# A second operand made from the x that is on chip: one core, two layers of a hybrid encoder

## The chip, the cores and the metric

One core of a Trainium2 chip runs the whole program. The metric is the device time of one execution in microseconds (us); the time before is the median of three runs.

## The reference

Two layers run over 512 frames of width 1024, all in fp32. Each layer has a first block with two branches, a feed-forward block, and a gated embedding. Cut to what matters here:

```python
for i in range(DEPTH):                       # DEPTH = 2
    h = rmsnorm(x, norm1_g[i])
    z = h @ w_in[i] + b_in[i]                # mLSTM q,k,v,o,i,f; retention q,k,v,g; gates gm, gr
    ...                                      # branch A: conv(q,k), mLSTM (4 heads), sig(o) * headnorm
    ...                                      # branch B: rotary q,k, retention (4 heads), silu(g) * headnorm
    merged = sigmoid(gm) * (y_m @ w_bm[i]) + sigmoid(gr) * (y_r @ w_br[i])
    x = x + merged @ w_out[i]
    h2 = rmsnorm(x, norm2_g[i])
    x = x + square(relu(h2 @ w_ff1[i] + b_ff1[i])) @ w_ff2[i] + b_ff2[i]
    h3 = rmsnorm(x, norm3_g[i])
    x = x + sigmoid(h3 @ w_pe_gate[i]) * (p[i] @ w_pe[i])
return rmsnorm(x, final_g)
```

## The kernel before

All activations lie transposed: x is eight tiles of 128 features by 512 frames (KT = 8, T = 512). Every fp32 operand of a matmul is split into a high and a low part in the matmul's reduced type, by a copy on ScalarE (ACT) and a subtraction on VectorE (DVE) (`split`, lines 262 and 263), and each product is three matmuls (`mm3`, lines 355 to 357). Weights stream in on the SyncE queue into a ring of four raw buffers and are split two units ahead of their use, into tiles wh and wl. `t8` is one output tile: eight k steps of three matmuls, 512 wide.

A group of eight projections (the retention queries, keys and gates, half of branch A's merge gates, all of branch B's, and the second feed-forward matrix) is done by pairs of tiles in a recursive seven-product scheme (`run_pair`). It needs sums and differences of quarters of the operand; for the branches these are the tiles xs (xsh, xsl), made by `xs_sums`, four batches of two tiles each.

In a layer's first block there are two versions of the normed x:

- The first operand xa is x times the norm's gain, without the norm's row factor (which is not known until all of x has been squared). Its results are multiplied by the row `n1.b` on the way out (the parameter `nrm`). It serves head 0, the values of heads 0 and 1, two branch gates (`gm_tile`) and head 1's queries and keys.
- The second operand xn is fully normed. `normed` loads a tile of x from memory on ACT's queue (line 935, tile xnr), multiplies it (line 936), and `xn_tile` splits it into xnh and xnl. Four tiles are made beside the two branch gates, four inside head 1's projection (lines 996 to 999). From head 0's output gates (`m_gates`) on, everything reads xn.
- `xs_sums` (lines 954 to 963) loads and multiplies x a second time (tile xsr), and all four batches stand behind the fourth head's values (lines 1028 and 1029).

`conv_evac` takes a query or key tile from PSUM: where `nrm` is given it multiplies it in place in PSUM (line 777), then ACT makes the first conv tap (line 778), and DVE adds three more (line 781).

At the end of the first block, `merged @ w_out` is added to x: line 1109 loads a tile of x into a temporary (xr), line 1111 adds, and the second norm's operand is made from the sum (n2h, n2l). After the last layer's gate the result is written out by `final`, which takes several tiles of x in one instruction.

Temporaries (`tmp`) come from a ring of NTMP = 6 tiles of 128x512 in this block; a tile is given out again when its last reader is done. The region "big" of 16 KB per partition holds x0, then the layer's xnh, then the layer's new x, each as one tile. The regions of xa, of xs and of the second norm's operand follow each other in one place.

The order on each engine is fixed when the program is built: a planner goes through the instructions in the order in which they are written, places them by its own estimate of times, and lets a later one go ahead where an earlier one can't start. In the trace, for instance, the loads of cos and sin (written behind the fourth head, line 1027) run in the first 10 us. GpSimd adds weight blocks in memory by DMA for the pair scheme, paced by the matmuls.

Of the kernel before, what the change touches and what calls it, by code (L numbers as in the profile page):

```python
# [35 lines left out]
F32 = mybir.dt.float32  # L36
F32R = mybir.dt.float32r
# [175 lines left out]
def build(ctx, tc, ins, out):  # L213
# [496 lines left out]
        return ct, em  # L710


    x = bpool.tile([P, KT, T], F32, name="x0", tag="big")
    xa_pool = phase("xa0", "right")
    cur["low"] = phase("low0", "left")
    cur["tmp"], cur["ntmp"] = cur["low"], NTMP
# [3 lines left out]
        te.matmul(warm[:, 0:P], ones, ones, start=True, stop=True)  # L720
    fill_raws(1)
    for k in range(KT):
        nc.sync.dma_start(x[:, k, :], ins["xT"][k])
    ready(0)
    for k in range(KT):
        n1.operand(k, x[:, k, :])
    nc.sync.dma_start(ident, ins["ident"])
    nc.sync.dma_start(bc[:, 1, :], ins["vecs"][1])

    for i in range(L):  # L730
# [37 lines left out]
            mm3(og, wh[:, s], wl[:, s], xa[0][k], xa[1][k], k == 0, k == KT - 1)  # L768
        if i == 0:
            for k in range(KT):  # L770
                n1.square(k, x[:, k, :])

        def conv_evac(o, nm, c, qh, ql, q, nrm):
            a = tmp(f"{nm}cv")
            cw = [bc[:, i, ow + 16 * j + c:ow + 16 * j + c + 1] for j in range(4)]
            if nrm:
                ve.tensor_tensor(o, o, nrm.b, OP.mult)
            ac.activation(a[:, :T], o, AF.Identity, bias=cbp[:, c:c + 1], scale=cw[3])
            for j in (2, 1, 0):
                t = slice(3 - j, T)  # L780
                ve.scalar_tensor_tensor(a[:, t], o[:, :T - 3 + j], cw[j], a[:, t], OP.mult, OP.add)
            ve.tensor_tensor(a[:, 0:3], a[:, 0:3], fix[:, :, c], OP.add)
            ac.activation(a[:, :T], a[:, :T], AF.Silu)
            if q:
                ac.activation(qh, a[:, :T], AF.Copy, scale=1.0 / 16)
                ve.scalar_tensor_tensor(ql, a[:, :T], 1.0 / 16, qh.bitcast(F32), OP.mult, OP.subtract)
            else:
                split(a[:, :T], qh, ql)
# [56 lines left out]
            head_scale(nm, num, 256, mv, hv)  # L845
            return num

        def m_gates(h):
            return [gated(f"l{i}m{h}o{v}", t8(xn, f"l{i}m{h}o{v}"), None, AF.Sigmoid, bcol(i, "bo", 2 * h + v))
                    for v in range(2)]  # L850

        def m_back(h, gs, num):
# [73 lines left out]
            nc.scalar.dma_start(gm_dram[i, c], g)  # L926


        big = bpool.tile([P, KT, T], F32R, name=f"l{i}xnh", tag="big")
        low = cur["br"].tile([P, KT, T], F32R, name=f"l{i}xnl", tag="xn")  # L930
        xn = [big[:, k, :] for k in range(KT)], [low[:, k, :] for k in range(KT)]

        def normed(nm, k):
            t = tmp(f"l{i}{nm}{k}")
            nc.scalar.dma_start(t, x_src[k])
            ve.scalar_tensor_tensor(t, t, n1.col(k), n1.b, OP.mult, OP.mult)
            return t

        def xn_tile(k):
            split(normed("xnr", k), xn[0][k], xn[1][k])  # L940

        def xs(k):
            def parts(j):
# [8 lines left out]
        xs = [xs(k) for k in range(4)]  # L952

        def xs_sums(k):
            t = [normed("xsr", 2 * k + a) for a in range(2)]
            u = [tmp(f"l{i}xsu{k}{a}") for a in range(2)]
            a, b = slice(0, S), slice(S, T)
            ve.tensor_tensor(u[0][:, a], t[0][:, b], t[0][:, a], OP.subtract)
            ve.tensor_tensor(u[0][:, b], t[1][:, a], t[0][:, a], OP.subtract)
            ve.scalar_tensor_tensor(u[1][:, a], u[0][:, b], -1.0, t[0][:, b], OP.mult, OP.subtract)  # L960
            ve.scalar_tensor_tensor(u[1][:, b], u[1][:, a], -1.0, t[1][:, b], OP.mult, OP.subtract)
            for a in range(2):
                split(u[a], xs_t[0][2 * k + a], xs_t[1][2 * k + a])
# [29 lines left out]
        gm = {}  # L993
        for c in range(2):
            gm_tile(c, xa, n1)
            xn_tile(2 * c)
            xn_tile(2 * c + 1)
        pt = m_scores(0, qk)
        qk = m_qk(1, xa, n1, lambda d: xn_tile(4 + d))
        xa_pool.release()  # L1000
        xs_pool = phase(f"xs{i}", act_side)
        shift(xs_pool, act_side, True)
        xs_t = acts(xs_pool, f"l{i}xs")
        shift(xs_pool, act_side, False)
        num = m_attend(0, pt, vv)
        gs = m_gates(0)
        gm_tile(2, xn, None)
        m_back(0, gs, num)
        pt = m_scores(1, qk)
        qk = m_qk(2, xn, None)  # L1010
        num = m_attend(1, pt, vv)
        gs = m_gates(1)
        vv = mv_vals(1, xn, None, lambda: m_back(1, gs, num))
        pt = m_scores(2, qk)
        qk = m_qk(3, xn, None)
        num = m_attend(2, pt, vv)
        gs = m_gates(2)
        gm_tile(3, xn, None)
        m_back(2, gs, num)
        pt = m_scores(3, qk)  # L1020
        gs = m_gates(3)
        num = m_attend(3, pt, vv)
        vv = rv_vals(0, lambda: m_back(3, gs, num))

        trig = [cur["low"].tile([P, T], F32, name=f"l{i}{n}", tag="trig", bufs=2) for n in ("cos", "sin")]
        for t, n in zip(trig, ("cos", "sin")):
            nc.scalar.dma_start(t, ins[n])
        for k in range(4):
            xs_sums(k)

        def bm_tile(c):
            if c < 4:
# [68 lines left out]
        xs_pool.release()  # L1101


        x = bpool.tile([P, KT, T], F32, name=f"l{i}x", tag="big")
        n2_pool = phase(f"n2{i}", act_side)
        n2 = Norm(f"l{i}n2", i, "g2", acts(n2_pool, f"l{i}n2"))
        for c in range(KT):
            xr = tmp(f"l{i}xr{c}")
            nc.scalar.dma_start(xr[:, :T], x_src[c])
            o = t8((mh, ml), f"l{i}wo{c}")  # L1110
            ve.tensor_tensor(x[:, c, :], o, xr[:, :T], OP.add)
            n2.tile(c, x[:, c, :])
        cur["low"].release()


# [28 lines left out]
            pair_operand(nm, st, *hid[b, p])  # L1144

        def tile3(c):
            n3.tile(c, x[:, c, :])

        def ff2(b, p):
            started = set()  # L1150

            def add(q, o, op):
                y = x[:, 2 * p + q // 2, (q % 2) * S:(q % 2 + 1) * S]
                if b == 0 and q not in started:
                    started.add(q)
                    ve.scalar_tensor_tensor(y, y, bcol(i, "bf2", 2 * p + q // 2), o, OP.add, op)
                else:
                    ve.tensor_tensor(y, y, o, op)

            def done(x_, o):  # L1160
                if x_ in ("P1", "P2"):
                    add(1, o, OP.add)
                elif x_ == "P5":
                    add(2, o, OP.subtract)
                elif x_ in ("P6", "P3"):
                    add(3, o, OP.subtract)
                elif x_ == "P7":
                    add(2, o, OP.subtract)
                elif x_ == "P4":
                    add(0, o, OP.add)  # L1170
                    if b == 3 and p == 3:
                        tile3(6)
                        tile3(7)
                if b == 3 and p and x_ in ("P6", "P7"):
                    tile3(2 * p - 2 + (x_ == "P7"))

            def parts(k):
                h, l = hid[b, k]
                return lambda j: (h[:, j * S:(j + 1) * S], l[:, j * S:(j + 1) * S])

            run_pair(f"l{i}o{b}{p}", [parts(k) for k in range(4)], done)
# [43 lines left out]
        def pe_evac(o, c, s, nn):  # L1225
            w = s.stop - s.start
            t = tmp(f"l{i}pgt{c}_{s.start}")[:, :w]
            ve.tensor_tensor(t, o[:, :w], n3.b[:, s], OP.mult)
            ac.activation(t, t, AF.Sigmoid)
            ve.tensor_tensor(t, t, pe[:, c, s], OP.mult)  # L1230
            ve.tensor_tensor(x[:, c, s], x[:, c, s], t, OP.add)
            for n in nn:
                if last:
                    n.square(c, x[:, c, :])
                else:
                    n.tile(c, x[:, c, :])

        for c in range(KT - LAST if last else KT):
            o = t8(n3.act, f"l{i}pg{c}")
            if c == 0:  # L1240
                n3.finish()
                held = o
                continue
            if c == 1:
                n3.spread()
                pe_evac(held, 0, slice(0, T), nn)
                if not last:
                    nc.scalar.dma_start(xs_dram[0], x[:, 0, :])
            pe_evac(o, c, slice(0, T), nn)
            if not last:  # L1250
                nc.scalar.dma_start(xs_dram[c], x[:, c, :])
        n1 = nn[0]
        if not last:
            cur["tmp"].release()
            n3_pool.release()

    def final(n, c0, c1):
        v = x[:, c0:c1, n.s]
        ve.tensor_tensor(v, v, n.b.rearrange("p (a t) -> p a t", a=1).to_broadcast([P, c1 - c0, n.n * P]), OP.mult)
        nc.sync.dma_start(out[c0:c1, :, n.s].rearrange("c p t -> p c t"), v)  # L1260

    for c in range(KT - LAST):
        ac.activation(x[:, c, :], x[:, c, :], AF.Copy, scale=nn[0].col(c))


    ws = [unit("T8") for _ in range(LAST)]
    for a, n in enumerate(nn):
        for c in range(KT - LAST, KT):
# [4 lines left out]
                mm3(o, wh[:, s], wl[:, s], n3.act[0][k][:, n.s], n3.act[1][k][:, n.s],  # L1273
                    k == 0, k == KT - 1)
            pe_evac(o, c, n.s, [n])
            ac.activation(x[:, c, n.s], x[:, c, n.s], AF.Copy, scale=n.col(c))
            if a == 1 and c == KT - LAST:
                nn[0].finish()
            elif a == 1 and c < KT - 1:
# [7 lines left out]
    cur["tmp"].release()  # L1287
    cur["last"].release()
    n3_pool.release()
    assert at["unit"] == NU and at["prep"] == len(order) and not pieces and not raws and at["load"] == len(order) and at["step"] == len(steps)  # L1290


# [111 lines left out]
```

## Time and profile before

| | before |
|---|---|
| median of three runs | 2447.42 us (2445.1 to 2448.85) |
| the profiled execution | 2447.46 us, span 2445.7 us |
| mean granted clock of TensorE | 0.983 |
| TensorE matmul busy | 97% |
| TensorE weight load busy | 86% |
| DVE busy | 65% |
| ACT busy | 49% |
| GpSimd busy | 10% |
| DMA | 481.9 MB, mean 197 GB/s |

Tile names carry the layer (l0, l1). PE is TensorE. In a row of the waits, the three numbers are the total wait in us, how often, and the longest. In a group of instructions stand busy us and mean ns, then the idle time of the engine before them and what ended it. A granted clock below 1.00 in a stretch means that TensorE ran part of it at half speed.

### The profile page before, as it was taken

Reading aid. Unit: us, or ns where it says so; the run is one execution under the profiler, and the core shown is the slowest. Engines: PE = TensorE matmul, PEld = TensorE weight load, DVE = VectorE, ACT = ScalarE, POOL = GpSimd, SP = SyncE. Lnnn points to the kernel's source line nnn. Section 1 sums busy time; section 2 is a strip of 40 time slices with the busy share of each in tenths; the row PEclk is TensorE's granted clock in tenths of the full one; section 3 lists DMA queues with packets and bytes.
Section 4 is the critical chain, followed back from the end, with each engine's and each line's share of the span. In section 5 each row is a group of like instructions: output and inputs, shape, how many; then the busy total and the mean of one; then the engine's idle time right before and its main releaser. Section 6 shows DMA issues by size and latency. Waiting matters only on the chain.

```text
span 2445.7 us, 35635 instructions
## 1 busy us (share of the span) xinstructions
PE 2378.4 (97%) x13788; PEld 2097.4 (86%) x13788; DVE 1589.8 (65%) x2451; ACT 1188.6 (49%) x1730; POOL 251.7 (10%) x368
## 2 busy tenths in 40 slices
PE   9899989999999999999999998999999999999997
PEld 7788878998998798899877886889989987998996
DVE  6766576774665577577777665667736655676675
ACT  5655443543454445445456552445535544455453
POOL 3121100000001100001301110000000010000012
PEclk9999999999999999999999999999999999999998
DMA  8666777668788777867767667776686884543441
GB/s 239 190 185 188 203 243 201 188 191 244 199 253 263 211 234 214 222 214 201 204 190 197 179 176 194 233 196 207 181 243 186 280 245 121 160 137 119 150 155 44
DMA packets 182187, 481.90 MB, mean 197 GB/s; under 512 B 18033, under 2 KB 20465, under 8 KB 182017
## 3 DMA queue, kind: packets, MB, share of 16 engines
q1 hardware_dynamic: 118512, 280.25, 34.5%
q0 software_dynamic: 41472, 159.39, 27.8%
q10 hardware_dynamic: 22032, 39.98, 4.7%
q8 instruction: 108, 1.77, 0.3%
q14 instruction: 63, 0.51, 0.1%
HBM read 464.87 MB, written 174.06 MB: 261 GB/s over the span
## 4 chain that ended last, share of the span: by engine, by line
PE 85%; DVE 5%; DMA 5%; issue 3%; ACT 1%; POOL 0%; ACTq 0%; POOLq 0%; DVEq 0%
PE l1f L356 2%; PE l1f L355 2%; PE l1f L357 2%; PE l0f L356 2%; PE l0f L357 2%; PE l0f L355 2%; PE l1br L357 1%; PE l0br L357 1%; PE l0br L355 1%; PE l1br L355 1%; PE l0br L356 1%; PE l1br L356 1%; DMA l1xsr<-x_spill 1%; DMA l1xr<-x_spill 1%; DMA l0xnr<-xT 1%
## 5 line engine op out<-in xcount | busy, mean ns | idle before, releaser
L262 ACT ACTIVATE wh<-wr 128x1024 fp32r<-128x1024 f32 x254 | 268.5, 1058 | 415.4 <-issue 46.1
L263 DVE TENSOR_TENSOR wl<-wr,wh 128x1024 fp32r<-128x1024 f32 x254 | 311.8, 1228 | 184.7 <-ACT wh L262 183.9
L262 ACT ACTIVATE wh_C<-wr 128x1024 fp32r<-128x1024 f32 x76 | 80.4, 1058 | 128.3 <-PE l0bm L356 8.8
L263 DVE TENSOR_TENSOR wl_B<-wr,wh_B 128x1024 fp32r<-128x1024 f32 x76 | 92.9, 1222 | 37.8 <-ACT wh_B L262 37.3
L262 ACT ACTIVATE wh_B<-wr 128x1024 fp32r<-128x1024 f32 x76 | 80.3, 1056 | 73.9 <-PE l1r1vp L572 4.2
L262 ACT ACTIVATE wh_D<-wr 128x512 fp32r<-128x512 f32 x76 | 47.9, 631 | 137.1 <-DMA wr<-s2t 13.9
L263 DVE TENSOR_TENSOR wl_D<-wr,wh_D 128x512 fp32r<-128x512 f32 x76 | 52.3, 688 | 95.7 <-ACT wh_D L262 93.2
L263 DVE TENSOR_TENSOR wl_A<-wr,wh_A 128x1024 fp32r<-128x1024 f32 x76 | 94.2, 1239 | 29.3 <-ACT wh_A L262 27.8
L263 DVE TENSOR_TENSOR wl_C<-wr,wh_C 128x1024 fp32r<-128x1024 f32 x76 | 92.9, 1222 | 29.2 <-ACT wh_C L262 27.2
L262 ACT ACTIVATE wh_A<-wr 128x1024 fp32r<-128x1024 f32 x76 | 80.2, 1055 | 54.4 <-PE l0f L356 11.3
L355 PE MATMUL l1f<-l1n2h,wh 128*128 128x512 f32 x256 | 100.9, 394 | 2.5 <-ACT l1n2h L477 2.5
L355 PE MATMUL l0f<-l0n2h,wh 128*128 128x512 f32 x256 | 100.9, 394 | 1.6 <-ACT l0n2h L477 1.6
L356 PE MATMUL l1f<-l1n2l,wh 128*128 128x512 f32 x256 | 100.7, 393 | 0.5 <-DVE l1n2l L478 0.5
L356 PE MATMUL l0f<-l0n2l,wh 128*128 128x512 f32 x256 | 100.7, 393 | 0.5 <-DVE l0n2l L478 0.5
L357 PE MATMUL l1f<-l1n2h,wl 128*128 128x512 f32 x256 | 100.6, 393 | 0.0
L357 PE MATMUL l0f<-l0n2h,wl 128*128 128x512 f32 x256 | 100.6, 393 | 0.0
L355 PEld LDWEIGHTS l1f<-l1n2h,wh 128*128 128x128 f32 x256 | 48.6, 190 | 12.7 <-ACT l1n2h L477 2.9
L355 PEld LDWEIGHTS l0f<-l0n2h,wh 128*128 128x128 f32 x256 | 48.6, 190 | 11.9 <-ACT l0n2h L477 2.0
L356 PEld LDWEIGHTS l0f<-l0n2l,wh 128*128 128x128 f32 x256 | 48.6, 190 | 10.8 <-DVE l0n2l L478 0.9
L356 PEld LDWEIGHTS l1f<-l1n2l,wh 128*128 128x128 f32 x256 | 48.6, 190 | 10.8 <-DVE l1n2l L478 0.9
L357 PEld LDWEIGHTS l0f<-l0n2h,wl 128*128 128x128 f32 x256 | 48.6, 190 | 10.3
L357 PEld LDWEIGHTS l1f<-l1n2h,wl 128*128 128x128 f32 x256 | 48.6, 190 | 10.3
(5445 smaller groups left out, 8266.0 us busy)
## 6 DMA issues: line engine op xcount, KB each, us to landing
wr<-wstream SPq DMA_DIRECT2D x254, 512.0 KB, 4.5
wr<-wpairs SPq DMA_DIRECT2D x228, 256.0 KB, 3.4
s0t<-wpairs POOLq DMA_DIRECT2D x6, 1024.0 KB, 10.0
s2t<-wpairs POOLq DMA_DIRECT2D x6, 1024.0 KB, 9.2
s3t<-wpairs POOLq DMA_DIRECT2D x6, 1024.0 KB, 9.2
s4t<-wpairs POOLq DMA_DIRECT2D x6, 1024.0 KB, 9.2
s5t<-wpairs POOLq DMA_DIRECT2D x6, 1024.0 KB, 9.1
s6t<-wpairs POOLq DMA_DIRECT2D x6, 1024.0 KB, 9.7
```

Of the source, the lines that this page charges most:

```text
L262: ac.activation(hi_ap, src, AF.Copy)
L263: ve.tensor_sub(lo_ap, src, hi_ap.bitcast(F32))
L355: te.matmul(o, sh, mh, start=first, stop=False)
L356: te.matmul(o, sh, ml, start=False, stop=False)
L357: cur["mm"] = te.matmul(o, sl, mh, start=False, stop=last)
```

## The change

- x0, the layer's xnh and the layer's x become eight tiles each in the region "big", so that a tile of xnh takes the place of its tile of x. The last layer's x lies whole in a region of its own on the side of the activations.
- `xn_tile` reads x from chip; the loads of xnr are gone. One tile is made behind head 0's scores, four inside head 1's projection, three behind head 0's output gates.
- Head 0's output gates and the third branch gate read xa and are multiplied by the norm's row.
- `xs_sums` adds xnh and xnl to get the normed tile back; the loads and products of xsr are gone. Its four batches stand behind head 2's projection, the second values, head 3's projection, and head 2's output.
- `conv_evac` writes the multiplied tile into a temporary z in place of PSUM, and the taps read z.
- The residual x is loaded into the tiles of the new x, all eight loads ahead of the output projection, and the sum is made in place.

```diff
-    x = bpool.tile([P, KT, T], F32, name="x0", tag="big")
+    def big(name, dt):
+
+        return [bpool.tile([P, T], dt, name=f"{name}{k}", tag="big", bufs=KT) for k in range(KT)]
+
+    x = big("x0", F32)
...
             if nrm:
-                ve.tensor_tensor(o, o, nrm.b, OP.mult)
+                z = tmp(f"{nm}z")
+                ve.tensor_tensor(z, o, nrm.b, OP.mult)
+                o = z
...
-        def m_gates(h):
-            return [gated(f"l{i}m{h}o{v}", t8(xn, f"l{i}m{h}o{v}"), None, AF.Sigmoid, bcol(i, "bo", 2 * h + v))
+        def m_gates(h, act, nrm):
+            return [gated(f"l{i}m{h}o{v}", t8(act, f"l{i}m{h}o{v}"), nrm, AF.Sigmoid, bcol(i, "bo", 2 * h + v))
...
-        big = bpool.tile([P, KT, T], F32R, name=f"l{i}xnh", tag="big")
         low = cur["br"].tile([P, KT, T], F32R, name=f"l{i}xnl", tag="xn")
-        xn = [big[:, k, :] for k in range(KT)], [low[:, k, :] for k in range(KT)]
-
-        def normed(nm, k):
-            t = tmp(f"l{i}{nm}{k}")
-            nc.scalar.dma_start(t, x_src[k])
-            ve.scalar_tensor_tensor(t, t, n1.col(k), n1.b, OP.mult, OP.mult)
-            return t
-
-        def xn_tile(k):
-            split(normed("xnr", k), xn[0][k], xn[1][k])
+        xn = [None] * KT, [low[:, k, :] for k in range(KT)]
+
+        def xn_tile(k, x=x):
+            t = tmp(f"l{i}xnr{k}")
+            ve.scalar_tensor_tensor(t, x[k], n1.col(k), n1.b, OP.mult, OP.mult)
+            xn[0][k] = bpool.tile([P, T], F32R, name=f"l{i}xnh{k}", tag="big", bufs=KT)
+            split(t, xn[0][k], xn[1][k])
...
         def xs_sums(k):
-            t = [normed("xsr", 2 * k + a) for a in range(2)]
+            t = [tmp(f"l{i}xsr{k}{a}") for a in range(2)]
+            for a in range(2):
+                ve.tensor_tensor(t[a], *[v[2 * k + a].bitcast(F32) for v in xn], OP.add)
...
             gm_tile(c, xa, n1)
-            xn_tile(2 * c)
-            xn_tile(2 * c + 1)
         pt = m_scores(0, qk)
-        qk = m_qk(1, xa, n1, lambda d: xn_tile(4 + d))
+        xn_tile(0)
+        qk = m_qk(1, xa, n1, lambda d: xn_tile(1 + d))
+        num = m_attend(0, pt, vv)
+        gs = m_gates(0, xa, n1)
+        for k in range(5, KT):
+            xn_tile(k)
+        gm_tile(2, xa, n1)
+        m_back(0, gs, num)
         xa_pool.release()
         xs_pool = phase(f"xs{i}", act_side)
...
-        num = m_attend(0, pt, vv)
-        gs = m_gates(0)
-        gm_tile(2, xn, None)
-        m_back(0, gs, num)
         pt = m_scores(1, qk)
         qk = m_qk(2, xn, None)
+        xs_sums(0)
         num = m_attend(1, pt, vv)
-        gs = m_gates(1)
+        gs = m_gates(1, xn, None)
         vv = mv_vals(1, xn, None, lambda: m_back(1, gs, num))
+        xs_sums(1)
         pt = m_scores(2, qk)
         qk = m_qk(3, xn, None)
+        xs_sums(2)
...
         m_back(2, gs, num)
+        xs_sums(3)
         pt = m_scores(3, qk)
...
-        for k in range(4):
-            xs_sums(k)
...
-        x = bpool.tile([P, KT, T], F32, name=f"l{i}x", tag="big")
+        if i == L - 1:
+            x_pool = phase("x", act_side)
+            whole = x_pool.tile([P, KT, T], F32, name=f"l{i}x", tag="x")
+            x = [whole[:, c, :] for c in range(KT)]
+        else:
+            x = big(f"l{i}x", F32)
+        for c in range(KT):
+            nc.scalar.dma_start(x[c], x_src[c])
...
         for c in range(KT):
-            xr = tmp(f"l{i}xr{c}")
-            nc.scalar.dma_start(xr[:, :T], x_src[c])
             o = t8((mh, ml), f"l{i}wo{c}")
-            ve.tensor_tensor(x[:, c, :], o, xr[:, :T], OP.add)
-            n2.tile(c, x[:, c, :])
+            ve.tensor_tensor(x[c], o, x[c], OP.add)
+            n2.tile(c, x[c])
```

All other uses of x change only in how a tile of it is named.

More of the change, by code (lines that the diff above doesn't have):

```diff
@@ L722, in build @@
     for k in range(KT):
-        nc.sync.dma_start(x[:, k, :], ins["xT"][k])
+        nc.sync.dma_start(x[k], ins["xT"][k])
     ready(0)
     for k in range(KT):
-        n1.operand(k, x[:, k, :])
+        n1.operand(k, x[k])
     nc.sync.dma_start(ident, ins["ident"])
@@ L770, in build @@
             for k in range(KT):
-                n1.square(k, x[:, k, :])
+                n1.square(k, x[k])
         def conv_evac(o, nm, c, qh, ql, q, nrm):
@@ L1004, in build @@
         shift(xs_pool, act_side, False)
-        num = m_attend(0, pt, vv)
-        gs = m_gates(0)
-        gm_tile(2, xn, None)
-        m_back(0, gs, num)
         pt = m_scores(1, qk)
         qk = m_qk(2, xn, None)
+        xs_sums(0)
         num = m_attend(1, pt, vv)
-        gs = m_gates(1)
+        gs = m_gates(1, xn, None)
         vv = mv_vals(1, xn, None, lambda: m_back(1, gs, num))
+        xs_sums(1)
         pt = m_scores(2, qk)
         qk = m_qk(3, xn, None)
+        xs_sums(2)
         num = m_attend(2, pt, vv)
-        gs = m_gates(2)
+        gs = m_gates(2, xn, None)
         gm_tile(3, xn, None)
         m_back(2, gs, num)
+        xs_sums(3)
         pt = m_scores(3, qk)
-        gs = m_gates(3)
+        gs = m_gates(3, xn, None)
         num = m_attend(3, pt, vv)
@@ L1146, in tile3 @@
         def tile3(c):
-            n3.tile(c, x[:, c, :])
+            n3.tile(c, x[c])
         def ff2(b, p):
@@ L1152, in add @@
             def add(q, o, op):
-                y = x[:, 2 * p + q // 2, (q % 2) * S:(q % 2 + 1) * S]
+                y = x[2 * p + q // 2][:, (q % 2) * S:(q % 2 + 1) * S]
                 if b == 0 and q not in started:
@@ L1230, in pe_evac @@
             ve.tensor_tensor(t, t, pe[:, c, s], OP.mult)
-            ve.tensor_tensor(x[:, c, s], x[:, c, s], t, OP.add)
+            ve.tensor_tensor(x[c][:, s], x[c][:, s], t, OP.add)
             for n in nn:
                 if last:
-                    n.square(c, x[:, c, :])
+                    n.square(c, x[c])
                 else:
-                    n.tile(c, x[:, c, :])
+                    n.tile(c, x[c])
         for c in range(KT - LAST if last else KT):
@@ L1247, in build @@
                 if not last:
-                    nc.scalar.dma_start(xs_dram[0], x[:, 0, :])
+                    nc.scalar.dma_start(xs_dram[0], x[0])
             pe_evac(o, c, slice(0, T), nn)
             if not last:
-                nc.scalar.dma_start(xs_dram[c], x[:, c, :])
+                nc.scalar.dma_start(xs_dram[c], x[c])
         n1 = nn[0]
@@ L1257, in final @@
     def final(n, c0, c1):
-        v = x[:, c0:c1, n.s]
+        v = whole[:, c0:c1, n.s]
         ve.tensor_tensor(v, v, n.b.rearrange("p (a t) -> p a t", a=1).to_broadcast([P, c1 - c0, n.n * P]), OP.mult)
@@ L1262, in build @@
     for c in range(KT - LAST):
-        ac.activation(x[:, c, :], x[:, c, :], AF.Copy, scale=nn[0].col(c))
+        ac.activation(x[c], x[c], AF.Copy, scale=nn[0].col(c))
     ws = [unit("T8") for _ in range(LAST)]
@@ L1275, in build @@
             pe_evac(o, c, n.s, [n])
-            ac.activation(x[:, c, n.s], x[:, c, n.s], AF.Copy, scale=n.col(c))
+            ac.activation(x[c][:, n.s], x[c][:, n.s], AF.Copy, scale=n.col(c))
             if a == 1 and c == KT - LAST:
@@ L1289, in build @@
     n3_pool.release()
+    x_pool.release()
     assert at["unit"] == NU and at["prep"] == len(order) and not pieces and not raws and at["load"] == len(order) and at["step"] == len(steps)
```

## The prediction

> **What bounds the kernel now.** I read the page first, then the waits of the TensorE (PE), then PE's own stretches around each wait.
>
> ```profile
> span 2445.7 us, 35635 instructions
> PE 2378.4 (97%) x13788; PEld 2097.4 (86%) x13788; DVE 1589.8 (65%) x2451; ACT 1188.6 (49%) x1730; POOL 251.7 (10%) x368
> ```
>
> PE is busy for 97% of the span, so the other engines matter only where PE waits for them. All that the change can win lies in such places, and the list of PE's waits is short:
>
> ```profile
> PE l1r0brqc L404 <- ACT l1xsh L262: 7.8, 2, 5.5
> PE l0r0brqa L404 <- ACT l0r0brqy L427: 4.4, 1, 4.4
> PE l0bgm L357 <- DVE wl L263: 4.1, 1, 4.1
> PE l0r0brqc L404 <- ACT l0xsh L262: 3.2, 1, 3.2
> PE l1f L355 <- ACT l1n2h L477: 2.5, 1, 2.5
> PE l0m0o L355 <- ACT l0xnh L262: 1.8, 1, 1.8
> PE l0f L355 <- ACT l0n2h L477: 1.6, 1, 1.6
> ```
>
> There are four places in each layer: the first branch gates (bgm, for a weight half wl), the output gates of head 0 (m0o, for the normed operand xnh and xnl), the first retention query pair (r0brq, for the operand sums xsh), and the first feed-forward tile (f, for the last norm tile n2h). The idle time is only part of the loss, because the granted clock falls behind it. So I compare stretches of PE. Columns: stretch, length, busy us (matmuls), granted clock, DMA share, GB/s.
>
> ```profile
> 140.00:157.00 17.00, 17.00 (x76) 1.00 0.68 207
> 470.00:480.00 10.00, 10.00 (x86) 1.00 0.63 195
> 111.00:128.00 17.00, 13.70 (x47) 0.80 0.51 113
> 1313.00:1330.00 17.00, 12.98 (x44) 0.80 0.50 110
> 310.00:327.00 17.00, 9.12 (x52) 0.70 0.86 262
> 1511.80:1538.00 26.20, 13.88 (x61) 0.61 0.69 231
> 815.50:827.00 11.50, 9.39 (x32) 0.73 0.64 149
> 2026.50:2038.00 11.50, 8.50 (x30) 0.76 0.32 104
> 63.00:74.00 11.00, 6.86 (x19) 0.69 0.51 162
> 1264.00:1275.00 11.00, 7.12 (x21) 0.69 0.33 116
> ```
>
> The first two rows are undisturbed and give the pace: 17.0/76 = 0.224 us for a matmul 512 wide, 10.0/86 = 0.116 us for one 256 wide. Loss = length minus matmuls times pace. Output gates of head 0: 17 - 47 x 0.224 = 6.5 and 17 - 44 x 0.224 = 7.2. Query pair: 17 - 52 x 0.116 = 10.9 and 26.2 - 61 x 0.116 = 19.1. The two feed-forward stretches hold eight narrow matmuls each (a norm's row sums), which take 0.79 us by the chain row below: 11.5 - 24 x 0.224 - 0.8 = 5.3 and 11.5 - 22 x 0.224 - 0.8 = 5.8. First branch gates: 11 - 19 x 0.224 = 6.7 and 11 - 21 x 0.224 = 6.3.
>
> Why PE waits there, from the chain, the instructions of line 936 and the loads' own rows:
>
> ```profile
> 27.98 0.79 PE l0n1ss L506 x8
> 317.96 4.09 DMA l0gml<-gm_spill
> 809.05 8.81 DMA l0xr<-xT
> ```
> ```profile
> L936 DVE SCALAR_TENSOR_TENSOR l0xnr<-l0xnr,bc,l0n1rb x8: 741/750/752, 87.4 to 124.7; 128x512 f32<-128x512 f32 x8
>   DMA l1xsr<-x_spill: 13.9, 5
>   DMA l1xnr<-x_spill: 10.6, 4
>   DMA l0xnr<-xT: 9.7, 4
> ```
> ```profile
> L1109 ACTq DMA_DIRECT2D l0xr<-xT x8: 334/334/339, 765.7 to 809.0; - x8
> ```
>
> The normed operand is made late because VectorE (DVE) sits 9.7 and 10.6 us waiting for x to come back from memory into one of six temporaries. The sums all come in one lump after the fourth head, wait for x again (13.9 us in layer 1), and hold the temporaries that the gate loads (gml) and the query results need; hence the 4.4 us wait for r0brqy. The last residual load is issued only at 809.05, when a temporary comes free, and lands 8.8 us later.
>
> **The change, part by part.**
>
> *Second operand from the x on chip.* Per layer 8 loads go (0.334 us each on ACT's queue). The 8 products (750 ns each) and both splits stay. The DVE waits of 9.7 and 10.6 us go; nothing takes their place, since x and the norm's row are there by the time head 0 is scored. The five later places are moved: head 0's gates and the third branch gate now read the first operand, so xn is needed only by head 2's projection, two tiles of gates, one of branch gate and a scoring later. Removed: 6.5 + 7.2 = 13.7 us. Added: three DVE products per layer with the norm's row (690 ns by the rows below, 2.1 us), beside PE. Cover: in 82 to 132 us DVE is busy 38.0 of 50, so 40.1 of some 43 to 50 after; if that cover is gone, 13.7 come back.
>
> ```profile
> 50.00:82.00 32.00, 28.07 (x53) 0.89 0.69 183
> 82.00:132.00 50.00, 37.99 (x73) 0.93 0.66 190
> 161.00:287.00 126.00, 71.12 (x137) 1.00 0.65 175
> ```
> ```profile
> L263 DVE TENSOR_TENSOR l0xsl<-l0xsu,l0xsh 128x512 fp32r<-128x512 f32 x8 | 5.5, 687 | 2.2 <-ACT l0xsh L262 2.1
> L777 DVE TENSOR_TENSOR l0m1z<-l0m1z,l0n1rb 128x512 f32<-128x512 f32 x4 | 2.8, 690 | 0.0
> L959 DVE TENSOR_TENSOR l0xsu<-l0xsr,l0xsr 128x256 f32<-128x256 f32 x4 | 1.7, 419 | 0.0
> L263 DVE TENSOR_TENSOR l0m0pl<-l0m0p,l0m0ph 128x512 fp32r<-128x512 f32 x1 | 0.8, 775 | 0.0
> ```
>
> *Sums from the two parts, spread over heads 1 to 3.* 8 more loads per layer go, 8 products become 8 additions (687 against 750 ns at best). One of the four batches is 2 x 0.69 + 4 x 0.42 + 2 x 0.69 = 4.4 us of DVE. All four in 161 to 287 us would make 71.1 + 17.7 = 88.8 of 126 us: there is room on average. Removed: 10.9 + 19.1 = 30.0 us at the query pair. Late next there: the gate loads of the four merge tiles, which now find free temporaries. If spread batches delay a head instead, see the rivals.
>
> *x read straight into place.* The same 8 loads per layer, but into x's own tiles. In layer 0 these are free once the last gate pair has read xn; in layer 1 they lie in a new region of 16 KB per partition where the sums were. All can go out about two tiles of PE (11 us) before the first is used, the later ones a tile of 24 x 0.224 = 5.4 us apart, against 8.8 us for the slowest landing now. Issued in a row they hold ACT's queue for 8 x 0.334 = 2.7 us, with weight halves behind them; those are made two units ahead, 10.8 us. Removed: 5.3 + 5.8 = 11.1 us. Bounds: 0 (loads still late) to 11.1; I take 11.1, since the wait is for that one row.
>
> *Conv input scaled into a temporary instead of in place in PSUM.* No instruction more, but each of 8 tiles per layer takes two temporaries, and the scaling now waits for one. Today it runs in between the gate arithmetic:
>
> ```profile
> 38.87 1.28 DVE L777 TENSOR_TENSOR l0m0z<-l0m0z,l0n1rb 128x512 f32<-128x512 f32 x2
> 52.73 1.19 DVE L676 TENSOR_TENSOR_SCAN l0gm<-l0glf,l0gli 4x512 f32<-4x512 f32 x1
> 57.23 0.73 DVE L781 SCALAR_TENSOR_TENSOR l0m00cv<-l0m0z,bc,l0m00cv 128x511 f32<-128x511 f32 x1
> 66.60 1.21 DVE L263 TENSOR_TENSOR wl<-wr,wh 128x1024 fp32r<-128x1024 f32 x1
> ```
> ```profile
> 51.43 1.06 ACT L262 ACTIVATE wh<-wr 128x1024 fp32r<-128x1024 f32 x1
> 56.44 0.78 ACT L778 ACTIVATE l0m02cv<-l0m0z,l0cbp,bc 128x512 f32<-128x512 f32 x1 [0.41 <-DVE l0grr L682]
> ```
>
> The third conv tile started only when line 682 gave up its temporary: the six are all in use. So the first scaling moves from 38.9 to some 54 us, behind the scan, and the conv chain then alternates between DVE and ACT with gaps. The weight half that PE waits for (wh ready at 52.5, wl made at 66.6, needed where that stretch begins, at 63) may fall into such a gap. Bounds for the two stalls at the first branch gates: all 13.0 us go, or 13.0 us more come if the convs themselves are late. I take half the gain, 6.5, because DVE in 50 to 82 us has only 3.9 us idle: order is what makes this wl late, and the order gets looser.
>
> [...]
>
> *What the spread adds.* Small new waits somewhere in the heads: from 0 to the price of one stall, 6.5; I take 3.
>
> **Sum.** The profiled execution took 2447.46 us (span 2445.7), and the median of the runs is 2447.42, so both stand alike. 13.7 + 30.0 + 11.1 = 54.8; 54.8 + 6.5 - 3 = 58.3; 2447.5 - 58.3 = 2389 us.
>
> [...]
>
> **Rivals.**
>
> *DVE becomes the bound in head 0.* With 40 us of work in as few as 43, with convs that queue for temporaries, xn comes late again and 13.7 us return: 2403 us. For it: DVE is already behind at 66.6. Against it: the 9.7 and 10.6 us of waiting disappear from the same stretch. Chance 0.13.
>
> *The residual loads are hidden no better.* Eight in one burst, 2 MB, land as late as now or hold up weight halves: 11.1 us stay, 2400 us. Against it: each has longer than its 8.8 us. Chance 0.07.
>
> *Some of the spread sums stall a head.* A batch holds four of six temporaries while scores and gates need them. Each stall costs what the others do with their slow clock, about 7 us. Two of eight: 2403 us. Chance 0.08.
>
> *The other side: all of them stall.* The same mechanism at every one of the eight places, from 58.3/8 = 7.3 us each on, makes the kernel slower; at 10 us each it gives 2389 + 80 = 2469 us. For it: the four temporaries, and the 4.4 us wait for r0brqy that came from just this. Against it: a load held each temporary then, for up to 8.8 us at worst, and a batch now has none. Chance 0.05; another 0.02 that it ends within 0.2%.
>
> **How the numbers follow.** The forecast has 0.65: 2389, with a range of its own from 2380 (first branch gates free) to 2398. The rivals to about 2403 hold 0.28 and lie on the same side of 2447. The range for 8 in 10 takes the better bound, 2378, and reaches past the single rivals to 2410. About 0.2% of the time, 5 us, is what can be told from no change; faster 0.93, same 0.02, slower 0.05.
>
> **What would show it.** In the profile after: no wait of PE for xnh, xnl, xsh or n2h; no wait of DVE for a load at the operand's product; 16 ACT loads fewer per layer; stretches at head 0's gates, at r0brq and at f at full granted clock; DVE busier between heads 1 and 3 and idle after the fourth. The wait of bgm for wl tells the open term. I am wrong if PE gets new waits for scores (the tiles ph, pl), for wl in heads 1 to 3, or for conv results, or if the f stretch still waits for x.

## The result, and the profile after

The changed kernel takes 2384.05 us (median of four runs, 2382.57 to 2390.69), the kernel before 2446.26 beside it: a ratio of 0.975, interval 0.9729 to 0.977. It is 62 us faster. 2389 was forecast, with 2378 to 2410 around it. The profiled execution of the changed kernel was its slowest run, 2390.69 us.

The page after, first lines of parts 1 and 3:

```profile
span 2388.9 us, 35583 instructions
PE 2354.4 (99%) x13788; PEld 2082.0 (87%) x13788; DVE 1588.6 (66%) x2457; ACT 1195.1 (50%) x1736; POOL 253.6 (11%) x368
DMA packets 177577, 473.50 MB, mean 198 GB/s; under 512 B 17520, under 2 KB 19952, under 8 KB 177408
```

PE has the same 13788 matmuls and is busy for 24 us less (2378.4 before), because fewer of them ran at half clock (the mean granted clock is 0.996, it was 0.983); the rest of the 57 us of span was idle time. The 8.4 MB that are gone are the 32 loads of 0.262 MB. DVE's busy time is what it was: nothing was won by doing less arithmetic.

The waits of PE after, the longest first, down to 0.9 us:

```profile
PE l1n41ss L508 <- ACT l1n41sq L491: 3.9, 1, 3.9
PE l1m0ot L628 <- DVE l1m0num L622: 2.4, 1, 2.4
PE l1r0brqa L404 <- ACT l1r0brqy L433: 2.3, 1, 2.3
...
PE l1m0s L355 <- ACT l1m0kh L262: 1.5, 1, 1.5
PE l1bgm2c L404 <- ACT l1bgm2y L429: 1.3, 1, 1.3
PE l0bgm2c L404 <- ACT l0bgm2y L429: 1.3, 1, 1.3
...
PE l0bgm L357 <- DVE wl L263: 1.0, 1, 1.0
PE l0wo L355 <- ACT l0mh L262: 0.9, 1, 0.9
```

No wait is left for xnh, xnl, xsh, xsl or n2h. The row n41ss belongs to the last norm, at the end of the program, and the two of bgm2c to the pair scheme; they were there before, as were the four rows left out. New are small ones in head 0 of layer 1 (m0ot, m0s) and at the output projection of layer 0 (wo), and one at layer 1's query pair, of which more below. Of the 4.1 and 3.9 us for wl at the first branch gates nothing is left. The 1.0 us in the row l0bgm lies at the third branch gate, as PE's own row shows:

```profile
116.23 0.50 PE L357 MATMUL l0bgm<-l0n1h,wl 128*128 128x512 f32 x1 [0.97 <-DVE wl L263]
```

The same places as in the prediction's table, in stretches of the same lengths (stretch, length, busy us and matmuls, granted clock, DMA share, GB/s): head 0's gates of both layers, the query pairs, the first feed-forward tiles, the first branch gates.

```profile
103.50:120.50 17.00, 16.03 (x73) 1.00 0.66 155
1280.00:1297.00 17.00, 16.60 (x75) 1.00 0.61 155
296.40:313.40 17.00, 16.91 (x140) 1.00 0.86 232
1474.10:1500.30 26.20, 23.34 (x176) 0.93 0.78 266
794.00:805.50 11.50, 11.50 (x56) 1.00 0.81 198
1975.00:1986.50 11.50, 11.50 (x56) 1.00 0.41 133
62.80:73.80 11.00, 11.00 (x50) 1.00 0.81 235
1237.40:1248.40 11.00, 11.00 (x50) 1.00 0.55 184
```

By the prediction's rule (length minus matmuls by pace) the gates of head 0 lose 17 - 73 x 0.224 = 0.6 (the wait at 116.23 us lies there) and 0.2 us, where they lost 6.5 and 7.2. The feed-forward and branch-gate stretches are full. Apart from that only layer 1's query pair still loses something, 26.2 - 176 x 0.116 = 5.8 us. ACT's own rows say why:

```profile
1483.43 1.06 ACT L262 ACTIVATE wh_B<-wr 128x1024 fp32r<-128x1024 f32 x1 [2.70 <-DMA wr<-s10t]
1484.39 0.36 ACT L433 ACTIVATE l1r0brqy<-l1r0brqa 128x256 f32<-128x256 f32 x1
```

A raw weight block (s10t) landed late, the copy wh_B waited for it, and the result brqy stood behind that copy in ACT's order. This has nothing to do with the sums, and it did not come again in the kernel's other profiled execution (after_again, below). So the changed kernel is better described by 2383 than by its own profile's 2390.7.

DVE shows the same from its side. Where it waited for the residual's load before (17.2 us in layer 1), it now waits for PE's products, which is as it should be:

```profile
DVE l1x L1123 <- PE l1wo L357: 19.4, 8, 2.7
```

And DVE's busy time in the three stretches of layer 0 that the prediction had counted, at the same clock times, though the program is up to 14 us further on in them:

```profile
50.00:82.00 32.00, 29.90 (x55) 1.00 0.78 209
82.00:132.00 50.00, 43.37 (x81) 1.00 0.61 170
161.00:287.00 126.00, 81.82 (x152) 1.00 0.71 200
```

### The profile page after: what moved, and what is told of

It is laid out like the page before. It is cut to its first block, busy times and chain, and to the rows that moved or that the text cites. A ratio compares the mean times of both kernels' runs of the same rounds, so it can differ in the third digit from the quotient of the medians.

```text
span 2388.9 us, 35583 instructions
## 1 busy us (share of the span) xinstructions
PE 2354.4 (99%) x13788; PEld 2082.0 (87%) x13788; DVE 1588.6 (66%) x2457; ACT 1195.1 (50%) x1736; POOL 253.6 (11%) x368
```

## The experiments

All times are medians; the ratio is to the kernel before on the same chip, with its interval. The changed kernel stands at 0.975 (0.9729 to 0.977) in its first comparison and at 0.9763 (0.9749 to 0.9776) when run once more. A distance in us from it is the difference of the medians. The kernel before took 2440.7 to 2447.2 us on the chips used, so the ratios give somewhat other distances; they are told where that matters.

### The temporary z, alone and taken away

z_alone is the kernel before with only this edit; no_z is the changed kernel without it.

```diff
-                ve.tensor_tensor(o, o, nrm.b, OP.mult)
+                z = tmp(f"{nm}z")
+                ve.tensor_tensor(z, o, nrm.b, OP.mult)
+                o = z
```

> The kernel before with one edit: the conv input goes through a temporary z. Theory (the order of DVE is looser, so the weight half of the first branch gates is made in a gap of the conv chain): both stalls at the first branch gates go, 6.7 + 6.3 = 13.0 us, and nothing else moves: 2434 us. Rival (these stalls went in the changed kernel because x no longer comes through the temporaries there, so DVE has less to do): nothing moves, 2447 us, and PE still waits 4 us for wl at bgm in each layer.

Measured: 2433.22 us, ratio 0.995 (0.9935 to 0.9966), 11 us faster than the kernel before it. At the first branch gates PE no longer waits in either layer. The 1.8 us that its list still has for wl lies at the third gate (122.3 us), and there is a new wait in layer 1 for a weight half of ACT:

```profile
PE l1m1z L355 <- ACT wh L262: 6.0, 1, 6.0
...
PE l0bgm L357 <- DVE wl L263: 1.8, 1, 1.8
```

So the forecast was right about the two stalls, and wrong in that nothing else would move: a wait of 6.0 us came, others shrank (at layer 1's first feed-forward tile from 2.5 to 0.8 us), and that the total came out as forecast is in part luck.

> The changed kernel with the conv input scaled in place in PSUM again. Theory as for z_alone: the two stalls at the first branch gates come back, 13 us: 2397 us. Rival: at most the small waits change, within 3 us of the changed kernel (2384).

Measured: 2391.86 us, ratio 0.9789 (0.9774 to 0.9804), some 8 us above the changed kernel (6 to 10 by the ratios). In no_z's waits of PE both of the old ones are back, as long as before:

```profile
PE l0bgm L357 <- DVE wl L263: 4.1, 1, 4.1
...
PE l1bgm L357 <- DVE wl L263: 3.9, 1, 3.9
```

The reason is the order on DVE. In the timeline of the changed kernel the weight half now runs between the first scaling and the first multiply-add, at 55.15 us; it ran at 66.60 before:

```profile
54.55 0.67 DVE L782 TENSOR_TENSOR l0m00z<-l0m0z,l0n1rb 128x512 f32<-128x512 f32 x1
55.15 1.20 DVE L263 TENSOR_TENSOR wl<-wr,wh 128x1024 fp32r<-128x1024 f32 x1
56.28 0.73 DVE L787 SCALAR_TENSOR_TENSOR l0m00cv<-l0m00z,bc,l0m00cv 128x511 f32<-128x511 f32 x1
```

With z the two stalls (13.0 us) go altogether, and by the medians some 5 us come back. The small waits fit that: in no_z the rows m0ot and m0s and the 1.0 us at the third branch gate are absent. So is the 0.9 us at wo, but that one is absent from after_again too, which has z.

### z for head 0 only

```diff
-                z = tmp(f"{nm}z")
+                z = tmp(f"{nm}z") if nm.startswith(f"l{i}m0") else o
```

> The changed kernel with the temporary z for head 0's conv tiles alone, head 1's scaled in place. Theory (z pays by letting a weight half pass between head 0's conv steps, and costs by its second temporary in head 1, where PE now waits 2.4 us at m0ot): faster than the changed kernel by 2 to 4 us, 2381 us. Rival (the small waits come from the tighter timing as such): same as the changed kernel within 2 us.

Measured: 2381.14 us, ratio 0.9732 (0.9701 to 0.9763). The forecast was right to the microsecond, and the wait at m0ot is gone from the list, while that at m0s stays: the first comes from the convs of head 1, the second from head 0's own. In return layer 1's third branch gate waits 1.2 us for wl. But the interval overlaps the changed kernel's, so the 3 us alone prove little.

### The second operand: the source, or the place

gates_on_xn keeps x on chip as the source but puts the tiles, and what head 0's gates read, back as they were:

```diff
             gm_tile(c, xa, n1)
+            xn_tile(2 * c)
+            xn_tile(2 * c + 1)
...
-        xn_tile(0)
-        qk = m_qk(1, xa, n1, lambda d: xn_tile(1 + d))
+        qk = m_qk(1, xa, n1, lambda d: xn_tile(4 + d))
...
-        gs = m_gates(0, xa, n1)
-        for k in range(5, KT):
-            xn_tile(k)
-        gm_tile(2, xa, n1)
+        gs = m_gates(0, xn, None)
+        gm_tile(2, xn, None)
```

> The changed kernel with the old places: the eight tiles of xn beside the first two branch gates and inside head 1's projection, and head 0's gates and the third branch gate on xn; x still comes from chip. Theory 1 (xn was late because its loads were): the stalls at head 0's gates stay away, 2384 us. Theory 2 (it was late because of its place: DVE has the convs of head 1 ahead of it, and the gates that read it come at once): both stalls come back whole, 13.7 us, 2398 us. Both: something between.

Measured: 2383.55 us, ratio 0.9745 (0.9719 to 0.9771), the same as the changed kernel. xn_loaded does the opposite: the new places, but each tile of x comes from memory again.

```diff
-            ve.scalar_tensor_tensor(t, x[k], n1.col(k), n1.b, OP.mult, OP.mult)
+            nc.scalar.dma_start(t, x_src[k])
+            ve.scalar_tensor_tensor(t, t, n1.col(k), n1.b, OP.mult, OP.mult)
```

> The changed kernel with its places, but each tile of xn is loaded from memory into its temporary again (16 loads more). Theory 1 (the loads): DVE waits for x some 10 us per layer again, and since DVE has about 3 us to spare there, stalls of 7 us per layer come back at head 2's projection or at a weight half: 2398 us. Theory 2 (the place): the first reader is 21 us later than before, more than the wait, so 2384 to 2387 us.

Measured: 2398.84 us, ratio 0.98 (0.9772 to 0.9827), 15 us above (9 to 12 by the ratios). The waits of PE in its profile, which is of an execution of 2392.91 us:

```profile
PE l1bgm L357 <- DVE wl L263: 7.2, 1, 7.2
...
PE l0bgm L357 <- DVE wl L263: 2.8, 1, 2.8
```

So the effect comes from the source; with x on chip, the new places add nothing. With the loads back, PE does not wait for xn at all (the gates no longer read it) but for a weight half behind it on DVE: DVE keeps its fixed order, and whatever follows the product that waits for the load (in all 4.6 us in layer 1, 3.1 in layer 0) is late. The stall is now at the third branch gate (1299.8 us in layer 1, 117.3 in layer 0).

### The operand sums: lump, load, or both

lump makes the sums from xnh and xnl, but all four batches behind the fourth head, as before:

```diff
-        xs_sums(0)
...
-        xs_sums(3)
...
+        for k in range(4):
+            xs_sums(k)
```

> The changed kernel with all four batches of operand sums back behind the fourth head's values; they are still made from the two parts on chip, with no load. Theory (the lump of DVE and ACT work and its hold on the temporaries stalls the query pair, whatever its source): 17.7 us of DVE work ahead of a pair that starts 22 us later, so 5 to 8 us of stall with the half clock in each layer, 2384 + 13 = 2397 us. Rival (only the loads made the lump late): the pair waits for nothing, 2384 us.

Measured: 2398.48 us, ratio 0.9814 (0.9794 to 0.9833), 14.4 us above (12 to 16 by the ratios). Its two longest waits of PE, and then ACT and DVE just ahead of the one in layer 0:

```profile
PE l1r0brqa L404 <- ACT l1r0brqy L427: 7.0, 1, 7.0
PE l0r0brqa L404 <- ACT l0r0brqy L427: 6.8, 1, 6.8
```
```profile
301.43 4.75 ACTq L1043 DMA_DIRECT2D bm_spill<-l0gml  x2
305.13 0.69 DVE L1042 TENSOR_TENSOR l0gml<-l0bm,l0gml 128x512 f32<-128x512 f32 x1 [3.73 <-DMA l0gml<-gm_spill]
306.28 0.38 ACT L427 ACTIVATE l0r0brqy<-l0r0brqa 128x256 f32<-128x256 f32 x1 [6.07 <-DVE l0gml L1042]
```

PE has the sums; it waits for the first result (brqy) to be taken out. That copy stands in ACT's order behind two transfers that store merge tiles (bm_spill). An issue alone takes 0.33 us; the row spans 4.75 us because the second one waited for DVE's product of a merge gate (gml), and DVE had waited 3.73 us for that gate's load. The loads of the gates went out late, the last two from 295.95 us on, just as the last batch of sums was done with its temporaries (295.9); the changed kernel had issued all four by 278 us. So the sums reach the result by way of the six temporaries that they share with the gates, and by ACT's order. That the loads waited for a temporary follows from these times; no row names it.

spread_loaded is the other half: the batches spread, but loaded and multiplied again.

```diff
-                ve.tensor_tensor(t[a], *[v[2 * k + a].bitcast(F32) for v in xn], OP.add)
+                nc.scalar.dma_start(t[a], x_src[2 * k + a])
+                ve.scalar_tensor_tensor(t[a], t[a], n1.col(2 * k + a), n1.b, OP.mult, OP.mult)
```

> The changed kernel with one thing put back: xs_sums loads its two tiles of x from memory and multiplies them by the norm again, as before; its four batches stay spread over heads 1 to 3. Of the 30.0 us at the query pairs, 14.4 came back when the sums were made on chip but in one lump; what the loads cost in the spread places isn't known. Theory 1 (the lump and its loads were two costs, and beside the heads a load has time to land, since no matmul waits for the sums before the query pair): no stall at r0brq, 2384 to 2387 us. Theory 2 (a load holds two temporaries until it lands and DVE waits for it in the fixed order, wherever it is): the other 15.6 us come back as waits of PE within heads 1 to 3, for ph, pl, wl or gates, about 2399 us.

Measured: 2386.39 us, ratio 0.9773 (0.9759 to 0.9786), 2.4 us above the changed kernel on the same chip, with intervals that overlap. No stall at r0brq. The same eight loads for which DVE waited 13.9 us in layer 1 before cost it 1.5 us here (from what is told of the tile l1xsr: DVE's wait, and the time from issue to landing):

```profile
  DMA l1xsr<-x_spill: 1.5, 2
DMA to landing us min/median/max: 2.5/3.0/4.5
```

So it is the place that counts here: lumped, even sums without a load stall; spread, the loads are hidden. In the kernel before they met.

### The residual

xr_back loads each tile of x into a temporary again, at its output tile.

```diff
-        for c in range(KT):
-            nc.scalar.dma_start(x[c], x_src[c])
...
+            xr = tmp(f"l{i}xr{c}")
+            nc.scalar.dma_start(xr[:, :T], x_src[c])
...
-            ve.tensor_tensor(x[c], o, x[c], OP.add)
+            ve.tensor_tensor(x[c], o, xr[:, :T], OP.add)
```

> The changed kernel with the residual x loaded into a temporary ahead of each output tile again, as before the change. Theory (the last load is issued when a temporary comes free and lands late): the stalls at the first feed-forward tile come back, 5.3 + 5.8 = 11.1 us less the 1.7 us that the burst of loads costs at the first output tile: 2384 + 9 = 2393 us. Rival (the stall went because the memory traffic of the first block fell and loads land sooner): within 3 us of 2384, and the last load lands in under 6 us.

Measured: 2391.31 us, ratio 0.9781 (0.9761 to 0.9801), 7 us above, though the interval touches the changed kernel's. Layer 1's stall is back in the profile (an execution of 2389.47 us), layer 0's is not. The wait, and the two stretches of PE (layer 1, then layer 0):

```profile
PE l1f L355 <- ACT l1n2h L477: 2.4, 1, 2.4
```
```profile
1968.00:1979.50 11.50, 8.52 (x28) 0.71 0.44 124
790.00:801.50 11.50, 11.50 (x56) 1.00 0.88 202
```

By the prediction's rule layer 1 loses 11.5 - 20 x 0.224 - 0.8 = 6.2 us: the price is that of one stall.

x_ahead asks whether eight loads in a row do harm:

```diff
-        for c in range(KT):
-            nc.scalar.dma_start(x[c], x_src[c])
...
+            if c == 0:
+                for k in range(3):
+                    nc.scalar.dma_start(x[k], x_src[k])
+            elif c + 2 < KT:
+                nc.scalar.dma_start(x[c + 2], x_src[c + 2])
```

> The changed kernel with three residual loads ahead of the output projection and the other five one by one, two tiles ahead of use. Theory (the burst of eight blocks ACT's queue for 4.5 us at 739 us, behind which the last gate pair's copy is late by 7.9 us and PE waits 1.1 us at the first output tile): that wait goes, and nothing comes back at the first feed-forward tile: 2 us faster, 2382 us. Rival (the planner issues the loads as early as before, or the last lands late): same or up to 6 us slower.

Measured: 2385.44 us, ratio 0.9752 (0.9724 to 0.9781), the same. The row was no loss, and the wait at wo that was to go is one that the changed kernel's second profile doesn't have either.

### Transfers that nobody waits for

```diff
+    scrap = tc.dram_tile([L, 2, KT, P, T], F32, name="scrap")
...
+            nc.scalar.dma_start(scrap[i, 0, k], x_src[k])
             t = tmp(f"l{i}xnr{k}")
...
             for a in range(2):
+                nc.scalar.dma_start(scrap[i, 1, 2 * k + a], x_src[2 * k + a])
```

> The changed kernel with 16 more transfers of an x tile per layer on ACT's queue, at the same places where the kernel before had its loads for the second operand and for the sums. They go from memory to an unused place in memory and nothing waits for them; so 16.8 MB are moved twice (read and written) in the whole program. Theory 1 (the old loads cost time only through what waited for them, not through the traffic or ACT's time to issue them): 2384 to 2386 us. Rival (the traffic itself delays weight blocks and other loads): 2390 us or more, with PE waits for wh or wl behind DMA.

Measured: 2392.51 us, ratio 0.9794 (0.978 to 0.9807), 8.5 us above. That is the rival's number but not its mechanism: no new wait of PE has a DMA of weights behind it. Nothing holds such a transfer back, so the planner did not leave them where they were written; the first row below has the eight of layer 0's second operand within the first 24 us. In layer 1 they ran into the time in which x was still being written; a row of two of them spans 6.18 us on ACT's queue, and ACT's copy n1h, behind them, made PE wait 3.0 us. In layer 0 the row of five of the sums' transfers spans 12.26 us, and ACT's copy of the norm's row, behind them, came at 40.87 us, where it came at 35.00 in the changed kernel.

```profile
L940 ACTq DMA_DIRECT2D scrap<-xT x8: 496/598/611, 1.2 to 23.7; - x8
```
```profile
27.93 12.26 ACTq L961 DMA_DIRECT2D scrap<-xT  x5
40.87 0.60 ACT L530 ACTIVATE l0n1rb<-l0n1rp 128x512 f32<-128x512 f32 x1 [11.89 <-DMA scrap<-xT]
...
1180.90 6.18 ACTq L940 DMA_DIRECT2D scrap<-x_spill  x2
...
1188.27 0.72 ACT L478 ACTIVATE l1n1h<-l0x,bc 128x512 fp32r<-128x512 f32 x1 [6.80 <-DMA scrap<-x_spill]
```
```profile
PE l1if L356 <- ACT l1n1h L478: 3.0, 1, 3.0
PE l0m0s L356 <- ACT l0m0kh L263: 2.8, 1, 2.8
```

The second row is a new wait in layer 0's first head, for a key tile from ACT. The late norm's row stands ahead of it, but the steps between were not followed. So the run doesn't answer the question it was made for. That the 8.4 MB themselves are worth little rests on spread_loaded, which has half of them at 2.4 us or less.

### The best of the runs together, and the changed kernel again

z_m0_gates_on_xn joins the edits of z_m0 and gates_on_xn; after_again is the changed kernel.

> The changed kernel with two things altered together: the temporary z only in head 0's convs (in place in PSUM elsewhere), and the second operand's tiles at their old places, with head 0's gates and the third branch gate reading it and not multiplied by the norm's row. Alone the first gave 2381.1 and the second 2383.6 us, against 2384.1. Theory 1 (the two are independent, and the places give nothing): 2380 to 2382 us. Rival (with the operand made earlier and the in-place convs of head 1, the weight half is late again at the first branch gates): the 13.0 us of bgm come back in part, 2386 us or more.

> The changed kernel itself once more, as the measure for the other runs on the same chip: 2384 us, 2382 to 2391. Two theories on its first profiled execution, which took 2390.7 where the others took 2383 to 2385: theory 1 (the wait of 2.3 us at layer 1's query pair behind a late piece of a weight, with 3.4 us at half clock, is an accident of one execution): an execution near 2383 has no such wait in its profile. Rival (it is always there): the same wait shows again.

Measured on one chip: 2380.34 us (2378.96 to 2383.89) for the first, ratio 0.975 (0.9737 to 0.9764), and 2384.04 us (2382.24 to 2385.27) for the second. The first is the fastest kernel of the study, by 3.7 us; the intervals overlap, so a small gain is likely rather than shown. The second's profile has full clock over layer 1's query pair and loses 26.2 - 217 x 0.116 = 1.0 us there, so the stall of the first profile is not a lasting trait of the kernel:

```profile
1472.80:1499.00 26.20, 26.11 (x217) 1.00 0.85 305
```

## Why the prediction was right, point by point

- **That only PE's stalls could be won**: right. DVE and ACT did as much work as before (1588.6 and 1195.1 us busy, where they had 1589.8 and 1188.6); the gain is PE's idle time and its half clock (mean granted clock 0.983 before, 0.996 after).
- **Second operand, 13.7 us**: right in size (xn_loaded gives back 15, or 9 to 12 by the ratios) and in the cause, the wait for the load. Wrong about the cover: the prediction counted the later places as a part of it, and gates_on_xn does without them. DVE's load in 82 to 132 us was put at 40.1 and is 43.37; the rival that DVE becomes the bound did not happen, since 6.6 us of the stretch stay free.
- **Sums, 30.0 us**: the size fits (of the 62 us measured, 15, 7 and 8 are accounted for by the other three edits, which leaves 32), but that is a remainder, and by the ratios it would be larger; a kernel with lump and loads together was not run. The split is new: 14.4 us are the lump alone, the loads alone cost 2.4 or less, and the rest arises only where both meet. The prediction named both causes without a split. The rival that spread batches stall a head did not happen, nor did its other side; DVE was forecast at 88.8 of 126 us there and had 81.8, but these two are not quite the same work: the first batch now begins at 152.9 us, ahead of the stretch.
- **Residual, 11.1 us**: too high, by the medians. 7 us came back, about those of layer 1 (4 to 8 by the ratios; the interval would still allow 11). In the one profile of xr_back layer 0 does not stall even with the temporaries: DVE still waits 6.4 us there for the loads, PE does not. The step that failed is the sum over two layers taken from the trace of before, with the wait for "that one row" in each. What had changed ahead of layer 0's last tile was not followed, so the cause stays open. The 8.8 us for the slowest landing were a piece of the chain; the view of the tile l0xr has 6.3 at most from issue to landing.
- **z, 6.5 us**: the open term, mis-sized. Alone it was worth 11, in the changed kernel 8: both stalls went, not half of them, and smaller waits came. The argument (a looser order lets wl run earlier) was right, as the row at 55.15 us shows.
- **New small waits, 3 us**: the right order of size, but not from the spread. In the first profile they were 2.4 and 1.5 us (m0ot, m0s) and 1.0 at the third branch gate, all absent without z, and 0.9 at wo, which comes and goes. The first two stay in lump, where nothing is spread. Without z in head 1 the kernel was 3 to 3.7 us faster by the medians. The wait at m0s is one for a conv result (the key tile), which the prediction had named as a sign of being wrong; it came, and cost little.
- **The convs' multiply-adds**: z was to add no instruction, and those that read it did not become longer. The three of the first conv tile took 728 ns each before, with the input in PSUM, and 730 after, with it in z (the two groups, before and after). The row l0m0pl that the prediction shows with 775 ns takes 779 after; what makes it longer than its like there (687) was not shown.

```profile
L781 DVE SCALAR_TENSOR_TENSOR l0m00cv<-l0m0z,bc,l0m00cv 128x511 f32<-128x511 f32 (+2 forms) x3 | 2.2, 728 | 0.0
```
```profile
L787 DVE SCALAR_TENSOR_TENSOR l0m00cv<-l0m00z,bc,l0m00cv 128x511 f32<-128x511 f32 (+2 forms) x3 | 2.2, 730 | 0.0
```

Altogether 58.3 us were forecast and 62 measured. By the runs z and its small waits, forecast at 6.5 - 3 = 3.5, gave 8 (4.5 more), the second operand 1 more, the sums 2 more (by the remainder), and the residual 4 less: the errors partly cancelled, and that the total came so close is in part luck.

## What to carry to other kernels

Where the matrix engine is 97% busy, list its waits, price each by the stretch behind it (time minus matmuls by pace), and ask of each what is late: three of the four here were a vector instruction that waited in its fixed order for a reload from memory, and in two of them the data were on chip already, as x or as its two parts. A reload was nearly harmless where nobody needed the result soon (2.4 us or less in spread_loaded), and cost more than its own wait where other work stood behind it (in xn_loaded DVE waited 7.7 us for the loads, and the time rose by 9 to 15); so spread first, and save the load second. Count who shares the temporaries: a new one taken in the wrong place (z in head 1) seems to have given back about a third of what the same one had won in head 0 (3 to 3.7 us, with intervals that overlap).

## What was not expected of the hardware

In these profiles, what a wait of PE costs behind it does not go by its length. In z_m0 a wait of 1.4 us at the output projection of layer 0 was followed by 3.4 us at half clock (stretches that hold the wait, the half clock, and full clock again):

```profile
749.00:752.00 3.00, 1.38 (x5) 1.00 1.00 399
752.00:755.40 3.40, 3.40 (x10) 0.50 0.44 158
755.40:758.80 3.40, 3.40 (x17) 1.00 0.33 123
```

In the first profile of the changed kernel a wait of 2.3 us ended at 1484.8 us with such a stretch behind it, and one of 2.4 us at 1299.0 without:

```profile
1485.60:1489.00 3.40, 3.40 (x18) 0.50 0.58 166
...
1299.00:1302.40 3.40, 3.40 (x19) 1.00 0.27 107
```

What decides whether a wait has half clock behind it, and for how long, no run here shows. For a forecast it means that a stall of one or two microseconds is a gamble for 1.7 us more (an estimate: half of the 3.4 us at half clock above), or for twice that (in traffic, at its wait of 3.0 us for n1h, a clock of 0.51 and 0.50 over two such stretches from 1197.6 us), and that one saved can bring more than its own length (the prediction's 4.1 us for wl in layer 0 stood for 6.7).
